# Moving the normed activations from 0 to 16 bytes modulo 64 in on-chip memory, in a two-layer decoder trunk

## The chip, the cores and the metric

The kernel runs on one core of one Trainium2 chip. The metric is the device time of one execution in microseconds (us). Three executions of the kernel before took 574.81, 575.57 and 575.68 us; the median is 575.57 us.

## What is computed

A sequence of 256 tokens with 1024 channels goes through one mLSTM layer, then shared keys and values are made from the stream, and then it goes through one attention layer with three branches. Cut to what matters here:

```python
h = rmsnorm(x, norm_pre[0])                       # hA in the kernel
xm, o_pre, z = split(h @ w_in, 3)                 # 1024 x 6144
... conv, block-diagonal q/k/v, gates, mlstm cell, head norm ...
x = x + rmsnorm(y @ a_w_out, norm_post[0])
kv = rmsnorm(x, kv_norm) @ kv_w                   # hK in the kernel
h = rmsnorm(x, norm_pre[1])                       # hB in the kernel
proj = h @ b_w_in                                 # 1024 x 8240: q, gates, three z branches
... compressed, selected and window attention, gated by silu(z) ...
x = x + rmsnorm(o @ b_w_out, norm_post[1])
```

All of it is float32.

## The kernel before

**Products in two parts.** A float32 product is made of two float32r parts per operand, `hi` and `lo` (`split`, L132: ScalarE copies to `hi`, VectorE subtracts to get `lo`). Each product is three matmuls (`mm3`, L137): L139 is hi by hi, L140 and L141 are the two mixed ones. A matmul of TensorE has a stationary operand of 128 columns, which a weight load (PEld) brings in beforehand, and a moving operand, which is streamed past it.

**Which operand moves.** In `proj_t` (L144) the weights `whi`/`wlo` are stationary and the normed activations `hA`, `hK` or `hB` move, 256 columns at a time; one call issues 2 x 8 x 3 = 48 matmuls into one PSUM tile. It makes `xmps` (L364 on), `zps`, `qps`, `xcps`, `ksps` and `kwps`; `branch_gates` (L784) makes `bgps` in the same way. In `o_gate` (L323) it is the other way round: `hA` is stationary and 512 columns of weights move. So it is in the values product of the keys/values stage (`vps`, L618), with `hK` stationary and `wv` moving, and in `OutProj.one` (L210), where the mixer's output (`y`, `ylow`, `yT`) is stationary and `whi`, `wlo` or `wl` moves.

**The order of the work.** Every engine works through its own program order. Weights come in chunks of 1024 elements per partition over the SyncE queue (`weights`, L115) into four rotating `raw` buffers and are split into five `whi` and four `wlo` buffers; the next chunks are loaded and split while TensorE works on the present one.

**The buffers that the change touches.** Pool `hp` has four buffers for tag `h8`. They hold in turn `hA` (hi and lo, `new_hT`, L193), the convolved activations `xc` (L320), two late weight chunks `wl` of the first output projection (`load_last`, L221), `hK`, `hB`, and the outputs `ylow` of the first three head pairs (L974). A tile starts where the allocator puts it, at a multiple of 32 bytes; a pool lies behind the one before it, and small `pad` tiles in the pools set where the next one starts. From the sizes and the order of the tiles, the start addresses of what TensorE reads, modulo 64 bytes, are these (slices of these tiles that the matmuls use start at multiples of 64 from there):

| operand | before | with the change |
|---|---|---|
| `hA`, `hK`, `hB` (hi and lo) | 0 | 16 |
| `xc` | 0 | 0 |
| `wl` (both) | 0 | 32 |
| `ylow` | 32 | 32 |
| `whi`, `wlo` | 32 | 32 |
| `y` of the first mixer, `yT`, `sd`, `v` of the cell | 32 | 32 |
| `wv`, `KT`, `V` | 0 | 0 |

Of the kernel before, what the change touches and what calls it, by code (L numbers as in the profile page):

```python
# [7 lines left out]
F32 = mybir.dt.float32  # L8
F32R = mybir.dt.float32r
# [6 lines left out]
P = 128  # L16
# [4 lines left out]
def trunk(ctx: ExitStack, tc: tile.TileContext, x, norm_pre, norm_post, a_w_in, a_conv_w, a_conv_b,  # L21
# [3 lines left out]
    S, D = x.shape[1], x.shape[2]  # L25
    NT = S // P
    KT = D // P
    AI = a_w_out.shape[1]
    AH = a_b_gate.shape[1] // 2
    ADH = AI // AH  # L30
    HT = ADH // P
# [11 lines left out]
    hp = ctx.enter_context(tc.tile_pool(name="hp", bufs=4))  # L43
# [53 lines left out]
    spare = []  # L97
# [81 lines left out]
    def norm_t(t, rstd, gam, hT):  # L179
# [10 lines left out]
            evac = split(hT[0][sl], hT[1][sl], ps)  # L190
        return ins.ins, *evac

    def new_hT(name):  # L193
        return [hp.tile([P, KT, S], F32R, tag="h8", name=f"{name}_{s}") for s in ("hi", "lo")]

    class OutProj:

# [22 lines left out]

        def load_last(self, k0, spare=0):  # L221

            homes = [[hp.tile([P, 2, 1024], F32R, tag="h8", name=f"wl{n}{k}") for n in range(2)] for k in range(0, spare, 2)]
            self.last = [(n, k, self.load(n, k, homes[(k - k0) // 2][n] if k < k0 + spare else None))
                         for k in range(k0, self.nk, 2) for n in range(2)]
            self.last.sort(key=lambda e: e[0])
# [19 lines left out]
    with ExitStack() as actx:  # L246
# [14 lines left out]
        nc.gpsimd.dma_start(out=rows[96:112], in_=a_skip[0].rearrange("(t p) -> t p", p=P))  # L261

        hT = new_hT("hA")
        keep_warm(8)
        gam_a = [wkt([P, 512], f"gam_a{n}") for n in range(2)]
# [51 lines left out]


        xm = [ah.tile([P, HT, S + 3], F32, tag="xm", name=f"xm{h}") for h in range(AH)]
        xc2 = [hp.tile([P, 2 * HT, S], F32, tag="h8", name=f"xc{h}") for h in range(AH // 2)]  # L320
        xc = [xc2[h // 2][:, h % 2 * HT:(h % 2 + 1) * HT, :] for h in range(AH)]
        for h in range(AH):
            nc.gpsimd.memset(xm[h][:, :, 0:3], 0.0)  # L323
# [40 lines left out]
        for j in range(NF // 2):  # L364
# [7 lines left out]
            h, j0 = divmod(2 * j, HT)  # L372
            nc.scalar.activation(xm[h][:, j0:j0 + 2, 3:], ps, AF.Copy)
            acc = a2.tile([P, 2, S], F32, tag="conv", name="conv")
            for m in range(2):
                f = 2 * j + m
# [211 lines left out]
        for c in range(4):  # L588
            n = wcount[0] = wcount[0] + 1
# [6 lines left out]
            vch.append([a.rearrange("p (k n) -> p k n", k=2) for a in hl])  # L596
        wv.tile([P, 120], F32, tag="pad", bufs=1, name="pad_wv")
        hK = new_hT("hK")
        rB, vps = [], []
        for t, n in op.finish():  # L600
            if n == 0:
                continue
            rB.append(rms_col(halves(xt[t])))
            with tc.high_priority(), tc.issue_after(op.near_end):
                ins = norm_t(t, rB[t], gam_k, hK)
            if t == 0:
                hold[:] = ins[2:]
            else:
                hold[:] = ins[0:2]
            vps.append(pjt([P, 512], f"vps{t}"))  # L610
            if t == 0:
                op_end = last_mm[0]
            with tc.issue_after(op_end):
                for c in range(4):
                    for k in range(2):
                        kk = 2 * c + k
                        mm3(vps[t], [a[:, kk, t * P:(t + 1) * P] for a in hK], [a[:, k, :] for a in vch[c]],
                            kk == 0, kk == KT - 1)  # L618
            if t == 0:
                hB = new_hT("hB")  # L620
            with tc.issue_after(last_mm[0]):
                norm_t(t, rB[t], gam_b, hB)
# [3 lines left out]
    with ExitStack() as bctx:  # L626
# [320 lines left out]
        def chunks(kv, c0, c1):  # L947
# [23 lines left out]
        pp = bctx.enter_context(tc.tile_pool(name="pp", bufs=7, side="right", reuse_waits="tile"))  # L971
        yp = bctx.enter_context(tc.tile_pool(name="yp", bufs=10, reuse_waits="tile"))
        yp.tile([P, 8], F32, tag="pad", bufs=1, name="pad_yT")
        ylow = [hp.tile([P, 4 * 2 * S], F32R, tag="h8", name=f"ylow{s}")[:, 56:56 + 3 * 2 * S].rearrange(  # L974
            "p (q i s) -> p q i s", q=3, i=2) for s in ("hi", "lo")]

        with tc.issue_after(after_norm):
# [58 lines left out]
```

## Time and profile before

| | |
|---|---|
| median of three executions | 575.57 us |
| the profiled execution, its own time | 574.73 us |
| its span from first to last instruction | 573.0 us |
| TensorE matmuls busy | 558.3 us (97%) |
| weight loads busy | 511.5 us (89%) |
| VectorE, ScalarE, GpSimd busy | 438.4, 316.8, 52.4 us |
| mean granted TensorE clock | 0.996 |

The profile is one execution. A matmul's own duration in it runs from its start to the modelled end of its passage through the array, and matmuls overlap; what one costs in a dense stream is therefore read from the distance between the starts of two that follow each other, over a run of many (starts are given to 0.01 us). Times are counted from the first instruction of the span.

### The profile page before, as it was taken

Reading aid. Unit: us, or ns where it says so; the run is one execution under the profiler, and the core shown is the slowest. Engines: PE = TensorE matmul, PEld = TensorE weight load, DVE = VectorE, ACT = ScalarE, POOL = GpSimd, SP = SyncE. Lnnn points to the kernel's source line nnn. Section 1 sums busy time; section 2 is a strip of 40 time slices with the busy share of each in tenths; the row PEclk is TensorE's granted clock in tenths of the full one; section 3 lists DMA queues with packets and bytes.
Section 4 is the critical chain, followed back from the end, with each engine's and each line's share of the span. In section 5 each row is a group of like instructions: output and inputs, shape, how many; then the busy total and the mean of one; then the engine's idle time right before and its main releaser. Section 6 shows DMA issues by size and latency. Waiting matters only on the chain.

```text
span 573.0 us, 10564 instructions
## 1 busy us (share of the span) xinstructions
PE 558.3 (97%) x4043; PEld 511.5 (89%) x4043; DVE 438.4 (77%) x927; ACT 316.8 (55%) x596; POOL 52.4 (9%) x88
## 2 busy tenths in 40 slices
PE   6999999999999999999999999999999999999995
PEld 2998987988999988879898999999999999998884
DVE  7679876485898876786625879888888888889563
ACT  6475777535544445464334766666666666666521
POOL 8623000101010040130000000000000000000000
PEclk9899999999999999999999999999999999999999
DMA  9995764253413447689996455555555545444501
GB/s 267 216 289 162 228 214 132 77 177 118 148 48 101 145 151 255 207 263 276 284 297 176 124 181 146 149 148 148 146 149 149 148 147 150 147 153 150 205 9 74
DMA packets 82693, 96.69 MB, mean 169 GB/s; under 512 B 4811, under 2 KB 68449, under 8 KB 82642
## 3 DMA queue, kind: packets, MB, share of 16 engines
q1 hardware_dynamic: 81040, 92.48, 52.9%
q0 software_dynamic: 1600, 3.52, 2.9%
q8 instruction: 32, 0.52, 0.4%
q14 instruction: 19, 0.16, 0.1%
q10 hardware_dynamic: 2, 0.00, 0.0%
HBM read 94.94 MB, written 1.05 MB: 168 GB/s over the span
## 4 chain that ended last, share of the span: by engine, by line
PE 84%; DMA 7%; DVE 4%; ACT 1%; issue 1%; SPq 1%; POOL 0%; DVEq 0%; POOLq 0%; ACTq 0%
PE zps L139 10%; PE zps L141 10%; PE zps L140 10%; PE acc L139 5%; PE acc L140 5%; PE acc L141 5%; DMA raw<-in_b_w_in_dram 4%; PE o L139 3%; PE o L140 2%; PE o L141 2%; PE xmps L141 2%; PE qps L139 2%; PE qps L141 2%; PE qps L140 2%; PE xmps L139 2%; PE xmps L140 2%
## 5 line engine op out<-in xcount | busy, mean ns | idle before, releaser
L135 DVE TENSOR_TENSOR wlo<-raw,whi 128x1024 fp32r<-128x1024 f32 x150 | 182.8, 1224 | 77.5 <-ACT whi L134 29.2
L134 ACT ACTIVATE whi<-raw 128x1024 fp32r<-128x1024 f32 x151 | 157.3, 1053 | 128.8 <-PE zps L140 28.2
L139 PE MATMUL zps<-hB_hi,whi 128*128 128x256 f32 x384 | 108.1, 282 | 0.0
L140 PE MATMUL zps<-hB_lo,whi 128*128 128x256 f32 x384 | 107.2, 279 | 0.0
L141 PE MATMUL zps<-hB_hi,wlo 128*128 128x256 f32 x384 | 107.1, 279 | 0.0
L139 PEld LDWEIGHTS zps<-hB_hi,whi 128*128 128x128 f32 x384 | 72.2, 188 | 0.8 <-ACT KThi L134 0.4
L140 PEld LDWEIGHTS zps<-hB_lo,whi 128*128 128x128 f32 x384 | 72.2, 188 | 0.0
L141 PEld LDWEIGHTS zps<-hB_hi,wlo 128*128 128x128 f32 x384 | 72.2, 188 | 0.0
L848 ACT ACTIVATE e<-e,nm 128x16 f32<-128x16 f32 (+2 forms) x96 | 38.0, 397 | 30.9 <-DVE nm L842 30.9
L141 PE MATMUL xmps<-hA_hi,wlo 128*128 128x256 f32 x128 | 36.8, 288 | 2.5 <-DVE wlo L135 2.5
L163 POOL TENSOR_TENSOR r<-u,mhalf 128x1 f32<-128x1 f32 x8 | 4.5, 562 | 350.8 <-DVE u L173 350.8
L139 PE MATMUL xmps<-hA_hi,whi 128*128 128x256 f32 x128 | 36.5, 285 | 0.0
L140 PE MATMUL xmps<-hA_lo,whi 128*128 128x256 f32 x128 | 36.4, 284 | 0.0
L139 PE MATMUL zps<-hA_hi,whi 128*128 128x256 f32 x128 | 36.1, 282 | 0.0
L141 PE MATMUL zps<-hA_hi,wlo 128*128 128x256 f32 x128 | 36.0, 281 | 0.0
L141 PE MATMUL qps<-hB_hi,wlo 128*128 128x256 f32 x128 | 35.7, 279 | 0.0
L139 PE MATMUL qps<-hB_hi,whi 128*128 128x256 f32 x128 | 35.7, 279 | 0.0
L140 PE MATMUL qps<-hB_lo,whi 128*128 128x256 f32 x128 | 35.7, 279 | 0.0
L140 PE MATMUL zps<-hA_lo,whi 128*128 128x256 f32 x128 | 35.7, 279 | 0.0
L141 PEld LDWEIGHTS xmps<-hA_hi,wlo 128*128 128x128 f32 x128 | 24.9, 194 | 2.9 <-DVE wlo L135 2.9
L381 DVE SCALAR_TENSOR_TENSOR conv<-xm,vec,conv 128x256 f32<-128x256 f32 x48 | 21.0, 479 | 6.3 <-ACT conv L378 6.2
L139 PE MATMUL o<-whi,hA_hi 128*128 128x512 f32 x64 | 25.6, 400 | 0.0
(337 smaller groups left out, 1397.9 us busy)
## 6 DMA issues: line engine op xcount, KB each, us to landing
raw<-in_b_w_in_dram SPq DMA_DIRECT2D x64, 512.0 KB, 4.9
raw<-in_a_w_in_dram SPq DMA_DIRECT2D x48, 512.0 KB, 4.7
raw<-in_a_w_out_dram SPq DMA_DIRECT2D x16, 512.0 KB, 3.5
w<-in_cmp_w_dram SPq DMA_DIRECT2D x32, 256.0 KB, 6.7
raw<-in_b_w_out_dram SPq DMA_DIRECT2D x16, 512.0 KB, 4.1
raw<-in_kv_w_dram SPq DMA_DIRECT2D x8, 512.0 KB, 5.8
raw<-in_kv_w_dram SPq DMA_DIRECT2D x8, 256.0 KB, 4.2
x<-in_x_dram SPq DMA_DIRECT2D x4, 256.0 KB, 3.7
```

The costliest lines, as they stand in the source:

```text
L134: a = nc.scalar.activation(hi, src, AF.Copy)
L135: return a.ins, nc.vector.tensor_sub(lo, src, hi.bitcast(F32)).ins
L139: nc.tensor.matmul(dst, lhsT=l[0], rhs=r[0], start=start, stop=False)
L140: nc.tensor.matmul(dst, lhsT=l[0], rhs=r[1], start=False, stop=False)
L141: last_mm[0] = nc.tensor.matmul(dst, lhsT=l[1], rhs=r[0], start=False, stop=stop).ins
L163: last_pow[0] = nc.gpsimd.tensor_tensor(r, u, mhalf[:, 0:n], op=ALU.pow)
L381: nc.vector.scalar_tensor_tensor(acc[:, m, :], src[:, k:k + S], vec[:, 16 * k + f:16 * k + f + 1], acc[:, m, :], op0=ALU.mult, op1=ALU.add)
L848: nc.scalar.activation(e[:, c0:c0 + n], e[:, c0:c0 + n], AF.Exp, bias=nm[:, i:i + 1], scale=-1.0, accum_out=sm[:, i:i + 1])
```

## The change

The four buffers get 16 float32 more (64 bytes), and each use takes its own place in them: the normed activations from element 4 (16 bytes), the late weight chunks from element 8 (32 bytes), `xc` from element 0 and `ylow` from element 56, as before. The second, third and fourth buffer thereby start 64, 128 and 192 bytes later, and all pools behind them on that side 256 bytes later, which leaves their addresses modulo 64 as they were. No instruction is added, removed or moved: on all five engines the order of instructions is the same before and after.

```diff
+    def buf8(name, dt):
+        return hp.tile([P, KT * S + 16], dt, tag="h8", name=name)
+
     def new_hT(name):
-        return [hp.tile([P, KT, S], F32R, tag="h8", name=f"{name}_{s}") for s in ("hi", "lo")]
+        return [buf8(f"{name}_{s}", F32R)[:, 4:4 + KT * S].rearrange("p (k s) -> p k s", k=KT) for s in ("hi", "lo")]
...
-            homes = [[hp.tile([P, 2, 1024], F32R, tag="h8", name=f"wl{n}{k}") for n in range(2)] for k in range(0, spare, 2)]
+            homes = [[buf8(f"wl{n}{k}", F32R)[:, 8:8 + 2048].rearrange("p (i n) -> p i n", i=2) for n in range(2)]
+                     for k in range(0, spare, 2)]
...
-        xc2 = [hp.tile([P, 2 * HT, S], F32, tag="h8", name=f"xc{h}") for h in range(AH // 2)]
+        xc2 = [buf8(f"xc{h}", F32)[:, 0:2 * HT * S].rearrange("p (j s) -> p j s", s=S) for h in range(AH // 2)]
...
-        ylow = [hp.tile([P, 4 * 2 * S], F32R, tag="h8", name=f"ylow{s}")[:, 56:56 + 3 * 2 * S].rearrange(
+        ylow = [buf8(f"ylow{s}", F32R)[:, 56:56 + 3 * 2 * S].rearrange(
             "p (q i s) -> p q i s", q=3, i=2) for s in ("hi", "lo")]
```

## Rows read from the trace of the kernel before

**Rows 1.** The page: busy time by engine, then the shares of the chain that ended last.

```profile
PE 558.3 (97%) x4043; PEld 511.5 (89%) x4043; DVE 438.4 (77%) x927; ACT 316.8 (55%) x596; POOL 52.4 (9%) x88
...
PE 84%; DMA 7%; DVE 4%; ACT 1%; issue 1%; SPq 1%; POOL 0%; DVEq 0%; POOLq 0%; ACTq 0%
```

**Rows 2.** TensorE's waits: who waited for whom, us in total, times, longest.

```profile
PE xmps L141 <- DVE wlo L135: 2.5, 2, 1.6
PE nT L188 <- DVE nrm L185: 2.0, 2, 1.1
```

**Rows 3.** Groups by line and shape: count, busy us, mean ns; L139 stands for L139 to L141.

```profile
L139 PE MATMUL zps<-hB_hi,whi 128*128 128x256 f32 x384 | 108.1, 282 | 0.0
...
L139 PE MATMUL xmps<-hA_hi,whi 128*128 128x256 f32 x128 | 36.5, 285 | 0.0
L139 PE MATMUL zps<-hA_hi,whi 128*128 128x256 f32 x128 | 36.1, 282 | 0.0
...
L139 PE MATMUL qps<-hB_hi,whi 128*128 128x256 f32 x128 | 35.7, 279 | 0.0
...
L139 PE MATMUL o<-whi,hA_hi 128*128 128x512 f32 x64 | 25.6, 400 | 0.0
...
L139 PE MATMUL xcps<-hK_hi,whi 128*128 128x256 f32 x32 | 9.0, 282 | 0.0
...
L139 PE MATMUL vps<-wvhi,hK_hi 128*128 128x512 f32 x16 | 6.3, 397 | 0.0
```

**Rows 4.** TensorE in order of time, one `proj_t` of the attention layer: start us, duration us.

```profile
339.28 0.28 PE L139 MATMUL zps<-hB_hi,whi 128*128 128x256 f32 x1
...
342.08 0.28 PE L139 MATMUL zps<-hB_hi,whi 128*128 128x256 f32 x1
```

**Rows 5.** The same view, `o_gate`: 512 columns of weights move, `hA` is stationary.

```profile
124.13 0.40 PE L139 MATMUL o<-whi,hA_hi 128*128 128x512 f32 x1
...
126.93 0.40 PE L139 MATMUL o<-whi,hA_hi 128*128 128x512 f32 x1
```

**Rows 6.** The same view, first output projection: weights in `whi`/`wlo`, then in `wl`.

```profile
228.97 0.39 PE L141 MATMUL acc<-whi,ylo 128*128 128x512 f32 x1
...
230.33 0.39 PE L141 MATMUL acc<-whi,ylo 128*128 128x512 f32 x1
230.56 0.40 PE L139 MATMUL acc<-wl,yhi 128*128 128x512 f32 x1
...
231.96 0.39 PE L139 MATMUL acc<-whi,yhi 128*128 128x512 f32 x1
```

**Rows 7.** The same view, second output projection and values product, 512 columns moving.

```profile
255.06 0.39 PE L139 MATMUL vps<-wvhi,hK_hi 128*128 128x512 f32 x1
...
257.10 0.39 PE L139 MATMUL vps<-wvhi,hK_hi 128*128 128x512 f32 x1
...
554.05 0.39 PE L139 MATMUL acc<-whi,yThi 128*128 128x512 f32 x1
...
565.61 0.39 PE L139 MATMUL acc<-whi,yThi 128*128 128x512 f32 x1
```

**Rows 8.** The same view: 12 transposes in one merged row; then their group, mean ns.

```profile
336.21 1.47 PE L873 MATMUL pt<-ident,e 128*128 128x128 f32 x12
...
L873 PE MATMUL pt<-ident,e 128*128 128x128 f32 x96 | 11.8, 273 | 0.0
```

**Rows 9.** The same view at the start, then busy time by stretch with the granted clock (PEclk).

```profile
15.51 0.41 PE L140 MATMUL xmps<-hA_lo,whi 128*128 128x256 f32 x1
...
18.07 0.41 PE L140 MATMUL xmps<-hA_lo,whi 128*128 128x256 f32 x1
...
core 0: us, PE busy (x) PEld busy (x) DVE busy (x) ACT busy (x) POOL busy (x), PEclk, DMA share, GB/s
15.50:18.00 2.50, 2.50 (x13) 2.50 (x13) 2.50 (x3) 0.30 (x1) 1.61 (x3) 0.50 1.18 69
```

**Rows 10.** Busy time by stretch, the same columns.

```profile
262.00:296.00 34.00, 34.00 (x333) 31.09 (x332) 16.73 (x17) 10.69 (x14) 0.00 (x0) 1.00 0.96 294
296.00:400.00 104.00, 103.53 (x892) 101.55 (x892) 82.25 (x217) 64.31 (x145) 0.00 (x0) 1.00 0.55 157
400.00:507.00 107.00, 107.00 (x890) 105.73 (x889) 92.83 (x256) 67.94 (x163) 0.00 (x0) 1.00 0.52 148
```

**Rows 11.** VectorE and ScalarE groups that write these buffers, and two on other places.

```profile
L135 DVE TENSOR_TENSOR ylo<-yt,yhi 128x512 fp32r<-128x512 f32 x8 | 5.4, 689 | 1.1 <-ACT yhi L134 0.9
L135 DVE TENSOR_TENSOR hB_lo<-nT,hB_hi 128x512 fp32r<-128x512 f32 x4 | 2.6, 680 | 0.0
L135 DVE TENSOR_TENSOR wl<-raw,wl 128x1024 fp32r<-128x1024 f32 x2 | 2.4, 1221 | 0.8 <-ACT wl L134 0.8
...
L134 ACT ACTIVATE yhi<-yt 128x512 fp32r<-128x512 f32 x8 | 4.9, 628 | 7.8 <-DVE yt L558 7.8
L134 ACT ACTIVATE hB_hi<-nT 128x512 fp32r<-128x512 f32 x4 | 2.3, 595 | 0.0
L134 ACT ACTIVATE wl<-raw 128x1024 fp32r<-128x1024 f32 x2 | 2.1, 1055 | 2.4 <-DMA raw<-in_a_w_out_dram 2.4
```

## The prediction

> **What bounds the kernel now.** I read the page first: TensorE's matmuls are busy for 97% of the span, and 84% of the chain that ended last is TensorE [rows 1]. Then its waits: the two longest sums are 2.5 and 2.0 us [rows 2]. So the span is a stream of matmuls with next to no holes in it, and its length is their number times the distance from one start to the next. The change leaves every instruction in its place; it can act only through that distance, or through the writes into the moved buffers. So the reader is to look at distances, by the kind of operands.
>
> *A product with the normed activations moving.* In one projection of the attention layer 24 matmuls lie between the starts at 339.28 and 342.08 us: 116.7 ns each, for 256 columns [rows 4]. Weights start at 32 modulo 64 there, activations at 0.
>
> [...]
>
> [...] In the first output projection, with the same stationary tiles and the same accumulators, six matmuls with weights in the rotating buffers (32 modulo 64, stationary y at 32) take 1.36 us, 226.7 ns each; the six behind them, whose weights lie in `wl` (0 modulo 64), take 1.40 us, 233.3 ns [rows 6]. The output gate, weights at 32 and stationary hA at 0, also takes 2.80 us for 12: 233.3 ns [rows 5]. The values product, both at 0, takes 2.04 us for 9: 226.7 ns, and the second output projection, both at 32, 11.56 us for 51: 226.7 ns [rows 7]. [...] A pair 16 bytes apart, which the change makes, is nowhere in this trace.
>
> **The change part by part.**
>
> *1. Projections, activations moving: 32 bytes apart becomes 16.* Three lines each of 384 + 128 + 128 + 128 + 32 matmuls [rows 3] make 2,400; `ksps` and `kwps` are one projection of 48 each and `bgps` 16: 2,512 in all, 293 us of the span at 116.7 ns. The price at 16 apart is not shown and is bounded. Below: every matmul here loads 128 new stationary columns, and 12 transposes that do no more than that for 128 moving columns take 1.47 us, the last of them 0.27: (1.47 - 0.27) / 11 = 109 ns apart [rows 8]. That is a floor: 2,512 x 7.7 = 19.3 us gained. [...] In between lies the price for equal places, half of 226.7, 113.3 ns: 8.4 us gained. I take the middle between the price at 0 apart (113.3) and at 32 apart (116.7), since 16 lies in the middle: 115.0 ns, a gain of 1.7 x 2,512 = 4.2 us.
>
> *2. Output gate, hA stationary: 192 matmuls, 32 apart becomes 16.* By the same middle 233.3 becomes 230.0: 0.6 us gained; bounds 0 to 1.3 gained (226.7), or the same 1.3 lost.
>
> *3. Values product, hK stationary: 48 matmuls, equal becomes 16 apart.* 226.7 becomes 230.0: 0.2 us lost; at 233.3 it is 0.3.
>
> *4. `wl` moving: 24 matmuls, 32 apart becomes equal.* 24 x 6.6 = 0.2 us gained; this one is measured on both sides [rows 6].
>
> *5. What cannot use the gain.* From 262 to 296 us the DMA engines are 96% busy [rows 10], with 256 of the 2,512 matmuls in it (xcps, ksps, kwps, bgps and the first q and z); weights set the pace there as soon as TensorE is quicker, so 0.4 us of part 1 is not had. Among the xm projections TensorE already waits 2.5 us for the lo split of the weights [rows 2]; I take half of their part (384 x 1.7 = 0.6) as lost, 0.3 us. In the attention stage the cover is there: VectorE is 79% busy from 296 to 400 us and 87% from 400 to 507 us [rows 10], ScalarE less, and a stream 1.4% shorter makes that 88% at most.
>
> *6. Writes and addresses.* Twelve evacuations each by ScalarE and VectorE write the moved activations. On a buffer at 0 they took 595 and 680 ns, the equal-sized ones of y at 32 628 and 689 ns [rows 11]: at most 33 ns by 12, 0.4 us, the lo parts 0.1 us; only those in the two norm stages are waited for, so I take 0 and keep 0.3 us for the range. The splits into `wl` (1055 and 1221 ns) are one-off and have TensorE's dense stream over them. The 64 and 192 bytes by which buffers move change addresses modulo 128 of half the tiles, `ylow` among them; no row separates that from modulo 64. Were `ylow`'s 72 matmuls to fall to 233.3, it would cost 0.5 us; I take 0.
>
> Sum: 4.2 + 0.6 - 0.2 + 0.2 - 0.7 = 4.1 us, so 574.73 becomes 570.6 for the profiled execution. That one stands 0.8 us below the median of three (575.57); between 570.6 and 571.5 I give **571.0 us**.
>
> [...] The rows say that where the two operands lie to each other is worth 6.6 ns on 512 columns. [...]
>
> **The rivals.**
>
> *A. No change (0.17): 575.2 us.* Only whether the two operands share a 32-byte place modulo 64 counts, and 16 apart costs what 32 apart costs. For: the trace knows two prices only. Parts 2 and 3 then give 0 and -0.3, part 4 +0.2. [...]
>
> *B. Slower (0.30): 583.5 us.* [...]
>
> *C. The whole gain (0.20, within "faster"): 566 us.* 16 apart is as good as equal or better: 113.3 ns, 8.4 + 1.3 + 0.2 = 9.9 us, less the uncovered part of it, about 1.4: 566.2. VectorE would then be 89% busy from 400 to 507 us, still not the bound. [...]
>
> **How the numbers follow.** Forecast (middle price) 0.33, C 0.20, A 0.17, B 0.30. About 0.2% (1.2 us) can be told from no change here; the cases lie on either side of that, so: faster 0.53, within 0.17, slower 0.30. Both signs hold much, and the range has to reach to C and to B: 562 to 584.5 us. What it leaves out is the floor price and a step larger than B's. The forecast's own range is 568 to 573.5 us (parts 1 and 2 between a third and two thirds of the way, part 6's 0.3 us and 0.8 us between execution and median).
>
> **What would show it.** Right: zps in the attention layer about 115 ns apart, the output gate at 230, acc from `wl` at 226.7, the values product at 230, the two output projections unchanged at 226.7, VectorE's share up by a point. Wrong: 116.7 again (A), 120 or more (B), 113 or less (C). A changed distance in acc with `whi` or in the second output projection would mean that more than these addresses counts; longer evacuations of hA, hK, hB, that the writes do; TensorE waiting for weights in the attention stage, that the gain was there and was taken by VectorE or the DMAs.

## The result, and the profile after

The kernel with the change takes 578.15 us (median of six executions, 577.79 to 579.17), the kernel before, beside it, 575.0 us (median of six). The ratio is 1.0061, 95% interval 1.0049 to 1.0072 (here and below the ratio is the one on record, which need not be the quotient of the two medians): slower by 3.2 us, against a forecast of 571.0, faster by 4. The profiled execution took 578.75 us with a span of 577.0, against 574.73 and 573.0.

The page of the kernel after, busy time by engine and then the shares of the chain that ended last, answers to [rows 1]:

```profile
PE 562.3 (97%) x4043; PEld 513.9 (89%) x4043; DVE 439.0 (76%) x927; ACT 316.6 (55%) x596; POOL 48.4 (8%) x88
...
PE 79%; DMA 9%; DVE 7%; ACT 2%; issue 1%; SPq 1%; POOL 0%; DVEq 0%; POOLq 0%; ACTq 0%
```

The same 4043 matmuls fill 97% of a longer span: 4.0 us more of busy TensorE, 4.0 us more of span. VectorE and ScalarE do the same work in the same time. The two waits that led before [rows 2]:

```profile
PE xmps L141 <- DVE wlo L135: 3.3, 5, 1.1
PE nT L188 <- DVE nrm L185: 1.9, 2, 1.2
```

They are no answer: the first is 0.8 us longer here, but in the slower kernels of this study it lies anywhere from 1.8 us (experiment 5, 578.86 us) to 3.6 (experiment 7, 580.88 us), and at 3.2 in the fastest (experiment 17, 574.2 us). Nor are the writes; the groups that answer to [rows 11]:

```profile
L135 DVE TENSOR_TENSOR hB_lo<-nT,hB_hi 128x512 fp32r<-128x512 f32 x4 | 2.6, 682 | 0.0
...
L134 ACT ACTIVATE hB_hi<-nT 128x512 fp32r<-128x512 f32 x4 | 2.3, 596 | 0.0
```

682 and 596 ns, where 680 and 595 stood. The stretch from 400 to 507 us has no hole, and fewer matmuls: 879, where [rows 10] had 890 in the same 107 us.

```profile
400.00:507.00 107.00, 107.00 (x879) 105.71 (x878) 92.01 (x253) 68.26 (x163) 0.00 (x0) 1.00 0.50 142
```

So the distance from matmul to matmul grew. TensorE in order of time (start us, duration us), the first and the last row of eight stretches of the kernel after:

```profile
110.17 0.28 PE L139 MATMUL zps<-hA_hi,whi 128*128 128x256 f32 x1
...
113.00 0.28 PE L139 MATMUL zps<-hA_hi,whi 128*128 128x256 f32 x1
...
124.55 0.40 PE L139 MATMUL o<-whi,hA_hi 128*128 128x512 f32 x1
...
127.33 0.40 PE L139 MATMUL o<-whi,hA_hi 128*128 128x512 f32 x1
...
227.76 0.39 PE L139 MATMUL acc<-wl,yhi 128*128 128x512 f32 x1
...
229.16 0.39 PE L139 MATMUL acc<-whi,yhi 128*128 128x512 f32 x1
...
231.90 0.39 PE L139 MATMUL acc<-wl,yhi 128*128 128x512 f32 x1
...
233.26 0.39 PE L139 MATMUL acc<-whi,yhi 128*128 128x512 f32 x1
...
254.89 0.39 PE L139 MATMUL vps<-wvhi,hK_hi 128*128 128x512 f32 x1
...
257.69 0.39 PE L139 MATMUL vps<-wvhi,hK_hi 128*128 128x512 f32 x1
...
340.72 0.28 PE L139 MATMUL zps<-hB_hi,whi 128*128 128x256 f32 x1
...
344.62 0.28 PE L139 MATMUL zps<-hB_hi,whi 128*128 128x256 f32 x1
...
530.15 0.39 PE L139 MATMUL acc<-whi,ylowhi 128*128 128x512 f32 x1
...
534.31 0.39 PE L139 MATMUL acc<-whi,ylowhi 128*128 128x512 f32 x1
...
558.07 0.39 PE L139 MATMUL acc<-whi,yThi 128*128 128x512 f32 x1
...
561.47 0.39 PE L139 MATMUL acc<-whi,yThi 128*128 128x512 f32 x1
```

| matmuls | in this stretch | ns apart | before | forecast |
|---|---|---|---|---|
| projections, hB moving | 33 in 3.90 us | 118.2 | 116.7 [rows 4] | 115.0 |
| projections, hA moving | 24 in 2.83 | 117.9 | 116.7 (45 in 5.25 from 108.45 us) | 115.0 |
| output gate, hA stationary | 12 in 2.78 | 231.7 | 233.3 [rows 5] | 230.0 |
| `wl` of the first column half | 6 in 1.40 | 233.3 | 233.3 [rows 6] | 226.7 |
| `wl` of the second | 6 in 1.36 | 226.7 | 233.3 | 226.7 |
| values product, hK stationary | 12 in 2.80 | 233.3 | 226.7 [rows 7] | 230.0 |
| output projection, `ylow` stationary | 18 in 4.16 | 231.1 | 226.7 (21 in 4.76 from 526.99 us) | 226.7 |
| output projection, `yT` stationary | 15 in 3.40 | 226.7 | 226.7 [rows 7] | 226.7 |

hB moves in 1,552 matmuls (3 x (384 + 128) for z and q, and 16 for `bgps`), hA in 768: 1,552 x 1.5 + 768 x 1.2 = 3.2 us lost. The 144 of `xcps` and `ksps`, hK moving, went from 116.7 to 117.8 ns, another 0.2 us. The small ones nearly cancel: `ylow` and the values product lose 0.3 us each, the output gate gains 0.3, `wl` 0.1. Sum 3.6 us, between the 3.2 of the medians and the 4.0 of the two spans.

Two of these rows say more than a size. The two `wl` halves now start at the same place modulo 64, and run at 233.3 and 226.7 ns. And `ylow`, whose address modulo 64 did not change at all, lost 4.4 ns. Modulo 64, in which the prediction counted, is too coarse. From the order and the sizes of the tiles the places are these, in bytes modulo 256: the weights `whi`, `wlo`, and `y`, `yT`, are at 224; before, every hi and lo part of hA, hK and hB was at 0 and both parts of `ylow` at 224. With the change a tile's hi and lo part lie in different buffers of the four, which start 64 bytes apart, so the two parts of each lie 64 apart modulo 128: at 16 and at 80. Modulo 256 the hi and the lo part of hA lie at 16 and 208, of hK at 16 and 80, and of hB, which moves in most of the matmuls, at 144 and 208. Of `ylow` the lo part stays with `y` modulo 128 and the hi part is 64 off; the first `wl` half is 64 off from `y` modulo 128, the second is level with it.

So the change had two parts that the prediction did not tell apart: the 16 bytes, and the 64 bytes of length that move the buffers and pull hi and lo apart.

### The profile page after: what moved, and what is told of

It reads as the page before. It is cut to its first block, busy times and chain, and to the rows that moved or that the text cites. A ratio compares the mean times of both kernels' runs of the same rounds, so it can differ in the third digit from the quotient of the medians.

```text
span 577.0 us, 10564 instructions
## 1 busy us (share of the span) xinstructions
PE 562.3 (97%) x4043; PEld 513.9 (89%) x4043; DVE 439.0 (76%) x927; ACT 316.6 (55%) x596; POOL 48.4 (8%) x88
## 3 DMA queue, kind: packets, MB, share of 16 engines
q0 software_dynamic: 1600, 3.52, 2.9%
## 4 chain that ended last, share of the span: by engine, by line
PE 79%; DMA 9%; DVE 7%; ACT 2%; issue 1%; SPq 1%; POOL 0%; DVEq 0%; POOLq 0%; ACTq 0%
PE zps L139 10%; PE zps L140 10%; PE zps L141 10%; PE acc L139 5%; PE acc L140 5%; PE acc L141 5%; DMA raw<-in_a_w_in_dram 3%; DMA raw<-in_b_w_in_dram 3%; PE qps L140 2%; PE qps L141 2%; PE qps L139 2%; PE o L139 2%; PE o L141 2%; PE o L140 2%; PE pt L877 2%; DVE wlo L135 2%
## 5 line engine op out<-in xcount | busy, mean ns | idle before, releaser
L139 PE MATMUL zps<-hB_hi,whi 128*128 128x256 f32 x384 | 108.2, 282 | 0.0
L141 PE MATMUL zps<-hB_hi,wlo 128*128 128x256 f32 x384 | 107.8, 281 | 0.0
L139 PEld LDWEIGHTS zps<-hB_hi,whi 128*128 128x128 f32 x384 | 72.6, 189 | 0.8 <-issue 0.4
L141 PEld LDWEIGHTS zps<-hB_hi,wlo 128*128 128x128 f32 x384 | 72.1, 188 | 0.0
L141 PE MATMUL xmps<-hA_hi,wlo 128*128 128x256 f32 x128 | 36.3, 284 | 3.3 <-DVE wlo L135 3.3
L139 PE MATMUL xmps<-hA_hi,whi 128*128 128x256 f32 x128 | 36.3, 284 | 0.3 <-ACT whi L134 0.2
L139 PE MATMUL zps<-hA_hi,whi 128*128 128x256 f32 x128 | 36.5, 285 | 0.0
L141 PE MATMUL qps<-hB_hi,wlo 128*128 128x256 f32 x128 | 36.0, 281 | 0.0
L141 PE MATMUL zps<-hA_hi,wlo 128*128 128x256 f32 x128 | 36.0, 281 | 0.0
L139 PE MATMUL qps<-hB_hi,whi 128*128 128x256 f32 x128 | 35.8, 279 | 0.0
L141 PEld LDWEIGHTS xmps<-hA_hi,wlo 128*128 128x128 f32 x128 | 24.0, 188 | 4.3 <-DVE wlo L135 4.3
L139 PE MATMUL o<-whi,hA_hi 128*128 128x512 f32 x64 | 25.6, 400 | 0.0
```

Of the source, the lines that this page charges most:

```text
L139: nc.tensor.matmul(dst, lhsT=l[0], rhs=r[0], start=start, stop=False)
L141: last_mm[0] = nc.tensor.matmul(dst, lhsT=l[1], rhs=r[0], start=False, stop=stop).ins
```

## The experiments

Diffs are against the kernel after, if nothing else is said, and some long lines end at `rearrange(`. "ns apart" is read as above, in the z projections of the attention layer (256 columns of hB moving), unless another product is named. Places are modulo 256, if nothing else is said. The "6.3%" of some expectations is over 213.3 ns for 512 columns, which is my estimate: 256 columns took 213.3 ns at a granted clock of 0.50 [rows 9], and I took the time as going with the number of columns and inversely with the clock. Of the weight load, which some expectations name, the trace of the kernel before gives this for the z projections of the attention layer: it takes 188 ns on average, longer than the 116.7 ns between two matmuls, and starts 0 to 0.01 us behind the matmul that runs beside it (339.17 us, the matmul at 339.16).

**1. The length without the 16 bytes.** Every use starts at element 0 of its longer buffer.

```diff
-        return [buf8(f"{name}_{s}", F32R)[:, 4:4 + KT * S].rearrange(
+        return [buf8(f"{name}_{s}", F32R)[:, 0:0 + KT * S].rearrange(
...
-            homes = [[buf8(f"wl{n}{k}", F32R)[:, 8:8 + 2048].rearrange(
+            homes = [[buf8(f"wl{n}{k}", F32R)[:, 0:0 + 2048].rearrange(
```

> Only the lengthening: the four buffers are 64 bytes longer, but the normed activations and the late weight chunks stay at element 0. Hi and lo tiles then lie 64 bytes apart modulo 128, everything stays as before modulo 64. Theory 1 (addresses count modulo 128, and the lengthening is what costs): projections of the attention layer at 118 ns instead of 116.7, the time 577 to 578.5 us, near the changed kernel. Theory 2 (the 16-byte start costs, the lengthening does not): 116.7 ns and 575 us, as before, but for the matmuls with ylow stationary, whose place is that of the changed kernel (231.5 ns instead of 226.7, 0.4 us).

578.03 us against 574.74: 1.0071 (1.0057 to 1.0085). TensorE in order of time in this kernel, hi and lo 64 apart:

```profile
411.87 0.29 PE L139 MATMUL zps<-hB_hi,whi 128*128 128x256 f32 x1
...
416.85 0.28 PE L139 MATMUL zps<-hB_hi,whi 128*128 128x256 f32 x1
```

42 in 4.98 us, 118.6 ns. Not one operand starts off a multiple of 32 bytes here, and the whole loss is there. The length is enough by itself. It puts hB at 128 (hi) and 192 (lo), hA at 0 and 192.

**2 to 4. Buffers of 128 bytes more, so that hi and lo agree modulo 128, with the activations at 16, 96 and 32 modulo 128.**

```diff
-    tp.tile([P, 72], F32, tag="pad", bufs=1, name="pad_h")
+    tp.tile([P, 8], F32, tag="pad", bufs=1, name="pad_h")
...
-        return hp.tile([P, KT * S + 16], dt, tag="h8", name=name)
+        return hp.tile([P, KT * S + 32], dt, tag="h8", name=name)
```

That alone is experiment 2, with the hi parts of the activations at 16 and the lo parts at 144; in 3 activations and `wl` start at element 24, in 4 the activations at 8 and `wl` at 24.

> Only the 16 bytes: buffers 128 bytes longer, so that every buffer starts at 0 modulo 128, normed activations at 16 modulo 128 in hi and lo alike; a pad before them is 256 bytes shorter to make room. Theory 1: the 16-byte start costs nothing, 115 to 116.7 ns, 571 to 575 us, ylow back at 226.7 ns. Theory 2: 118 ns and 577 to 578.5 us. If addresses count modulo 256 too, ylow stays near 231 ns, since its hi and lo tiles now lie 128 bytes apart modulo 256.

> Normed activations and late weight chunks at 96 modulo 128, the place of the weights, in every buffer. If 256 moving columns follow the same law as 512 (6.3% over at equal places): 113.3 ns, output gate 226.7, values product 233, late weight chunks 226.7, 565 to 567 us. If the weight load, which lasts through the whole of a 256-column matmul, makes equal places no better there: 116 ns or more, 574 to 580 us, with the output gate at 226.7 all the same. If modulo 256 counts, one of the two late weight chunks stays at 233.

> Normed activations at 32 modulo 128: equal to the weights modulo 64, 64 bytes apart modulo 128. A law modulo 64 gives what e3 gives, 113.3 ns and 566 us if that law holds for 256 columns. A law modulo 128 in which 64 apart costs what 32 apart costs, as the late weight chunks of the changed kernel show for 512 columns: 116.7 ns, output gate 233, 574 to 576 us.

At 16: 577.62 us, 1.0048 (1.0036 to 1.0061), 117.7 ns (39 in 4.59 us). At 96: 581.92, 1.0125 (1.0111 to 1.0139), 119.6 ns (27 in 3.23). At 32: 576.6, 1.0033 (1.002 to 1.0046), 117.1 ns (45 in 5.27). At 96 activations and weights agree modulo 128, and that is the slowest of the three, against every expectation built on equal places. And `ylow`, whose two parts agree modulo 128 and differ by 128 modulo 256, got slower still; the row view of experiment 2:

```profile
527.14 0.40 PE L139 MATMUL acc<-whi,ylowhi 128*128 128x512 f32 x1
...
533.44 0.39 PE L139 MATMUL acc<-whi,ylowhi 128*128 128x512 f32 x1
```

27 in 6.30 us, 233.3 ns, where before had 226.7. Modulo 128 does not do either.

**5 and 6. The 128 bytes with everything at 0; then the same buffers with the places put back.** Experiment 5 is experiment 2 with activations and `wl` at element 0: hi parts at 0, as in the kernel before, lo parts at 128. Experiment 6 starts the part of each tile that lies 128 bytes off 32 elements later (the lo part; of `ylow` the hi part), which makes good the 128 bytes. Its diff against experiment 5:

```diff
-        return [buf8(f"{name}_{s}", F32R)[:, 0:0 + KT * S].rearrange("p (k s) -> p k s", k=KT) for s in ("hi", "lo")]
+        return [buf8(f"{name}_{s}", F32R)[:, o:o + KT * S].rearrange("p (k s) -> p k s", k=KT) for s, o in (("hi", 0), ("lo", 32))]
...
-            homes = [[buf8(f"wl{n}{k}", F32R)[:, 0:0 + 2048].rearrange(
+            homes = [[buf8(f"wl{n}{k}", F32R)[:, 32 * n:32 * n + 2048].rearrange(
...
-        ylow = [buf8(f"ylow{s}", F32R)[:, 56:56 + 3 * 2 * S].rearrange(
+        ylow = [buf8(f"ylow{s}", F32R)[:, o:o + 3 * 2 * S].rearrange(
...
+            for s, o in (("hi", 88), ("lo", 56))]
```

> Buffers 128 bytes longer as in the run at 16, but the normed activations and late weight chunks at element 0: that run without its 16 bytes. Theory 1, now modulo 256 (what costs is that the hi and lo tiles no longer lie at the same place modulo 256): 117.6 to 118 ns in the attention layer's projections and 577 us, as there. Theory 2 (there the 16 bytes cost): 116.8 ns, 575 us.

> The same longer buffers, with the lo tiles (and the second late weight chunk, and ylow's hi tile) 128 bytes further into theirs, so that hi and lo lie at the same place modulo 256 again. Theory 1: back to 116.8 ns, ylow back to 227, 574.7 us although the buffers are longer. If addresses count modulo 512 too: the mLSTM projections, whose hi and lo agree modulo 512 here, are back at 116.8, those of the attention layer, 256 bytes apart modulo 512, stay at 117.6. Rival (the length or the shifted pads cost by themselves): 117.6 everywhere, 577 us.

Experiment 5: 578.86 us, 1.0061 (1.0037 to 1.0085), zps up to 118.7 ns (30 in 3.56 us), `ylow` 233.3 (21 in 4.90). Experiment 6: 574.79 us against 574.88, 0.9995 (0.9981 to 1.0008). Its rows:

```profile
410.93 0.28 PE L139 MATMUL zps<-hB_hi,whi 128*128 128x256 f32 x1
...
415.83 0.28 PE L139 MATMUL zps<-hB_hi,whi 128*128 128x256 f32 x1
...
527.21 0.39 PE L139 MATMUL acc<-whi,ylowhi 128*128 128x512 f32 x1
...
533.33 0.39 PE L139 MATMUL acc<-whi,ylowhi 128*128 128x512 f32 x1
```

42 in 4.90 us, 116.7 ns, and 27 in 6.12 us, 226.7 ns: both back where they were. The length itself costs nothing; what costs is the places modulo 256 that it gives the tiles. In experiment 5 only the lo parts had left 0, and yet the step from one matmul with a hi part moving to the next (L141 to L139) grew as well, from 116.7 to 117.9 ns on average in the z projections. How much of the loss is the place of the moved part and how much its distance from the other is not shown: with both parts at 128 (experiment 10) the price is 117.3 or 118.7 ns. In experiment 6 the parts of hA agree modulo 512 as well and those of hB and hK do not, and all are back, so 256 is enough.

**7 and 8. No longer buffers; all four buffers moved as one, to 224 (the weights' own place) and to 32.** The first diff is against the kernel before; for 32 the pad in `hp` has 8 elements, `pad_s` keeps 48, and `ylow` starts at 48.

```diff
-    sp.tile([P, 56], F32, tag="pad", bufs=1, name="pad_s")
+    hp.tile([P, 56], F32, tag="pad", bufs=1, name="pad_hp")
...
-        ylow = [hp.tile([P, 4 * 2 * S], F32R, tag="h8", name=f"ylow{s}")[:, 56:56 + 3 * 2 * S].rearrange(
+        ylow = [hp.tile([P, 4 * 2 * S], F32R, tag="h8", name=f"ylow{s}")[:, 0:0 + 3 * 2 * S].rearrange(
```

> Buffers as long as before, all four moved by 224 bytes (a pad goes from behind them to ahead of them), ylow's offset taken back: the normed activations lie at 224 modulo 256, exactly where the weights lie, hi and lo alike. The law of my forecast (equal places cost 6.3%): 113.3 ns, output gate 226.7, 565 to 567 us. Rival (at 256 columns the weight load runs through the whole matmul, and equal places collide): 119 ns or more, 578 us or more, with the output gate at 226.7 nevertheless.

> Buffers as long as before, all four moved by 32 bytes, ylow's offset taken back: the normed activations at 32 modulo 256, hi and lo alike. If only their common place counts, whatever it is: 116.8 ns, 574 to 575 us. If the distance from the weights (224, now 64 bytes away around 256 instead of 32) sets the price: another price, 113 to 120 ns, 566 to 583 us, the output gate moved too.

At 224: 580.88 us, 1.0094 (1.0071 to 1.0116). Its rows:

```profile
125.40 0.39 PE L139 MATMUL o<-whi,hA_hi 128*128 128x512 f32 x1
...
127.44 0.39 PE L139 MATMUL o<-whi,hA_hi 128*128 128x512 f32 x1
...
414.41 0.28 PE L139 MATMUL zps<-hB_hi,whi 128*128 128x256 f32 x1
...
416.93 0.28 PE L139 MATMUL zps<-hB_hi,whi 128*128 128x256 f32 x1
```

This pair of stretches refutes the prediction's step from 512 columns to 256. Equal places give the output gate its 226.7 ns (9 in 2.04 us; 228.2 on average over the whole gate), as [rows 7] promised for 512 columns; and the same equal places give 256 columns 120.0 ns (21 in 2.52 us), not the 113.3 that is half of it, and worse than the 116.7 at 32 apart. At 32 everywhere: 576.52 us, 1.0025 (1.001 to 1.004), 117.8 ns (45 in 5.30), but one projection ran 42 matmuls in 4.76 us from 433.85 us on, 113.3 ns; the output gate stayed at 233.3, which the second theory had moving.

**9. The 16 bytes without any split.** Buffers of 256 bytes more keep hi and lo at one place; activations at 16, the late weight chunks at 224 like `y`, all other operands where they were modulo 256.

```diff
-    tp.tile([P, 72], F32, tag="pad", bufs=1, name="pad_h")
-    sp.tile([P, 56], F32, tag="pad", bufs=1, name="pad_s")
+    tp.tile([P, 8], F32, tag="pad", bufs=1, name="pad_h")
...
-        return hp.tile([P, KT * S + 16], dt, tag="h8", name=name)
+        return hp.tile([P, KT * S + 64], dt, tag="h8", name=name)
...
-            homes = [[buf8(f"wl{n}{k}", F32R)[:, 8:8 + 2048].rearrange(
+            homes = [[buf8(f"wl{n}{k}", F32R)[:, 56:56 + 2048].rearrange(
...
-        ap.tile([P, 104], F32, name="pad_y")
+        ap.tile([P, 32], F32, name="pad_y")
...
+        bp.tile([P, 56], F32, name="pad_b")
```

> The 16 bytes alone: buffers 256 bytes longer, so that all four start at 0 modulo 256, normed activations at 16 modulo 256 in hi and lo alike, late weight chunks at 224 (equal to the y tiles); pads elsewhere shortened so that all other places modulo 256 stay. If the split of hi and lo by 64 bytes is the whole loss of the changed kernel: 116.8 ns, 574.5 to 575.5 us. If the 16 bytes cost too: 117.5 ns or more, 576 us or more. My forecast's middle price would be 115 ns, 570.5 us.

578.12 us against 574.32: 1.0063 (1.0049 to 1.0077). Its rows:

```profile
412.84 0.28 PE L139 MATMUL zps<-hB_hi,whi 128*128 128x256 f32 x1
...
416.75 0.28 PE L139 MATMUL zps<-hB_hi,whi 128*128 128x256 f32 x1
```

33 in 3.91 us, 118.5 ns. So the 16 bytes alone cost what the length alone costs, and both together (578.15) no more than either. Together they put hB at 144 and 208, a place of neither experiment, so there was no sum to expect. The output gate, with both parts of hA at 16:

```profile
124.09 0.40 PE L139 MATMUL o<-whi,hA_hi 128*128 128x512 f32 x1
...
126.89 0.40 PE L139 MATMUL o<-whi,hA_hi 128*128 128x512 f32 x1
```

12 in 2.80 us, 233.3 ns, the price before: for the gate the 16 bytes bring nothing. The values product, with hK at 16, ran one of its two halves at 226.7 ns and the other at 233.3.

**10 to 16 and 18. Other places in the family of experiment 9.** Only the element at which hA, hK and hB start differs (4 there). Each ran once, so their times are compared only by whole microseconds; the distances are read from the trace. The kernel before took 574.32 us beside 9 to 12, 575.04 (one run) beside 13 to 16 and 574.99 beside 18.

> The same with the activations at 128 modulo 256, 96 bytes below the weights at 224. If every place but the weights' own costs the same: 116.8 to 117.7 ns, 574 to 577 us. If the price falls with distance: below 116.7 ns, 566 to 573 us.

> The same at 192 modulo 256, 32 bytes below the weights, where the kernel before lies 32 bytes above them (0 against 224). If only the size of the distance counts: 116.8 ns, 575 us. If its sign counts, since the weight load starts a few ns behind the matmul: another price, 113 to 120 ns, 566 to 583 us.

> The same at 240 modulo 256, 16 bytes above the weights: between the equal place (120.0 ns) and 32 above (116.8). A price that falls evenly with distance: 118.4 ns, 579 us. If a start off a multiple of 32 costs: over 120 ns, 583 us or more.

> Activations at 248 modulo 256, 24 bytes above the weights, hi and lo alike. At 240 a projection ran at one of three steady distances (113.3, 116.7, 118.7 ns). Theory 3 (the distance of the places sets which rhythms exist, and what ran before picks one): other rhythms than at 240, 113.3 to 118.7 ns, 566 to 579 us. [...]

> The same at 232, 8 bytes above the weights, near the equal place with its one rhythm of 120.0 ns. [...]

> The same at 208, 16 bytes below the weights: the distance of 240 with the other sign. If the sign does not count: 113.3 to 118.7 ns in a mixture, 575 to 578 us. If it does, as between 192 (118.1) and 0 (116.8): one rhythm, 117 to 120 ns, 576 to 581 us.

> [...]

> All normed activations at 216 modulo 256, 8 bytes below the weights: 16 below gave 117.1 ns with the output gate at 228.3, 0 gave 120.0, 8 above a mixture of 117.6 and 120.0. A price that moves evenly: 118.5 ns, output gate 227.5, 577 us. If the rhythm of 113.3 is the only one here: 566 to 568 us.

"Behind" is at a higher address than the weights, "ahead" at a lower one, counted around 256.

| experiment | activations at | from the weights (224) | us | ns apart |
|---|---|---|---|---|
| (before) | 0 | 32 behind | 575.0 | 116.7 |
| 9 | 16 | 48 behind | 578.12 | 118.5 |
| 8 | 32 | 64 behind | 576.52 | 117.8, once 113.3 |
| 10 | 128 | 96 ahead | 578.05 | 117.3 or 118.7 |
| 11 | 192 | 32 ahead | 578.48 | 118.1 |
| 15 | 208 | 16 ahead | 574.32 | 117.3 |
| 18 | 216 | 8 ahead | 581.62 | 120.0 |
| 7 | 224 | equal | 580.88 | 120.0 |
| 14 | 232 | 8 behind | 576.5 | 117.6 or 120.0 |
| 16 | 236 | 12 behind | 576.68 | 117.6 |
| 12 | 240 | 16 behind | 577.61 | 113.3, 116.7 or 118.7 |
| 13 | 248 | 24 behind | 582.07 | 120.0 |

Neither the distance from the weights nor its sign orders this list: 8 ahead, equal and 24 behind share the worst price, and 16 ahead is nearly as good as 32 behind. Experiment 18 was a plain miss: no theory that I had gave its 120.0 ns; the times of 10, 12, 13 and 15 lay outside what was expected too. The step of 8 bytes from 208 (experiment 15, first two rows) to 216 (experiment 18):

```profile
410.90 0.28 PE L139 MATMUL zps<-hB_hi,whi 128*128 128x256 f32 x1
...
414.42 0.28 PE L139 MATMUL zps<-hB_hi,whi 128*128 128x256 f32 x1
...
410.87 0.28 PE L139 MATMUL zps<-hB_hi,whi 128*128 128x256 f32 x1
...
413.39 0.28 PE L139 MATMUL zps<-hB_hi,whi 128*128 128x256 f32 x1
```

30 in 3.52 us and 21 in 2.52, 117.3 and 120.0 ns. The output gate averages 228.4 ns at 208, as low as at the equal place (228.2), and 233.3 at 216. Experiment 12 holds three prices in one execution; its rows:

```profile
142.39 0.28 PE L139 MATMUL zps<-hA_hi,whi 128*128 128x256 f32 x1
...
147.49 0.28 PE L139 MATMUL zps<-hA_hi,whi 128*128 128x256 f32 x1
...
164.95 0.28 PE L139 MATMUL zps<-hA_hi,whi 128*128 128x256 f32 x1
...
169.50 0.28 PE L139 MATMUL zps<-hA_hi,whi 128*128 128x256 f32 x1
...
383.91 0.28 PE L139 MATMUL zps<-hB_hi,whi 128*128 128x256 f32 x1
...
388.90 0.28 PE L139 MATMUL zps<-hB_hi,whi 128*128 128x256 f32 x1
```

45 in 5.10 us, 39 in 4.55 and 42 in 4.99: 113.3, 116.7 and 118.8 ns, the same operands at the same places each time. A projection falls into one steady distance and keeps it.

**17. A place for each tile: hA at 208, hK and hB at 0.** As experiment 9, with

```diff
-        return [buf8(f"{name}_{s}", F32R)[:, 4:4 + KT * S].rearrange("p (k s) -> p k s", k=KT) for s in ("hi", "lo")]
+        return [buf8(f"{name}_{s}", F32R)[:, 52 * (name == "hA"):52 * (name == "hA") + KT * S].rearrange(
+            "p (k s) -> p k s", k=KT) for s in ("hi", "lo")]
```

> Put together from the places read so far: hA alone at 208 modulo 256, where the output gate took 228.3 ns instead of 233.4 and the projections 117.1 instead of 116.9; hK and hB at 0 as before; late weight chunks at 224. 192 x 5.1 = 1.0 us and 24 x 7 = 0.2 us gained, 768 x 0.2 = 0.2 us lost: 573.9 us against 574.9, 0.2% faster than the kernel before. Theory 3 holds if hB and hK are back at 116.7 ns beside it; if places were tied across tiles, hB would leave 116.7.

574.2 us against 574.99: 0.9986 (0.9974 to 0.9998), 0.8 us less than the kernel before, close to the expected 573.9 and barely clear of no change. Its rows:

```profile
123.32 0.39 PE L139 MATMUL o<-whi,hA_hi 128*128 128x512 f32 x1
...
126.75 0.39 PE L139 MATMUL o<-whi,hA_hi 128*128 128x512 f32 x1
...
410.87 0.28 PE L139 MATMUL zps<-hB_hi,whi 128*128 128x256 f32 x1
...
415.07 0.28 PE L139 MATMUL zps<-hB_hi,whi 128*128 128x256 f32 x1
```

The output gate runs at 228.7 ns (15 in 3.43 us), 4.6 less than before on 192 matmuls, 0.9 us; hB at 0 is back at 116.7 (36 in 4.20). A tile's place prices the products that read it, and leaves the others alone.

## Why the prediction was wrong

**What held.** TensorE's stream is the bound and nothing covers it: matmuls times the change of their distance give 3.6 us, where 3.2 to 4.0 us were lost. The edit acts through addresses alone; writes cost nothing (682 and 596 ns beside 680 and 595, part 6), neither VectorE (439.0 us busy beside 438.4) nor the weights took a part, the output projection from `yT` stayed at 226.7. One half of `wl` came to 226.7 (part 4, 0.1 for 0.2).

**What came out by luck.** The output gate did gain (part 2, 0.3 us of the 0.6) and the values product did lose (part 3, 0.3 for 0.2), but not by a middle price at 16. With both parts of hA at 16 the gate takes 233.3 ns, no gain, and the values product with hK at 16 keeps 226.7 in one half (experiment 9). In the changed kernel the lo part of hA lies at 208 and that of hK at 80, which the prediction did not count; at 208 the gate averages 228.4 ns (experiment 15).

**The step that failed is part 1,** 4.2 us gained, measured as 3.4 us lost on hA, hB and hK. Three things in it were wrong, each with its run.

*Half the price of 512 columns was taken for that of 256.* "In between lies the price for equal places, half of 226.7, 113.3 ns": experiment 7 has equal places at both widths, 226.7 ns at 512 and 120.0 at 256. I built that step on one agreement of two numbers: at 32 apart, 116.7 ns and 233.3 ns are both 9.4% over an estimate of mine, 106.7 ns for 256 columns (half of the 213.3 ns at a granted clock of 0.50 [rows 9]) and 213.3 ns for 512. No run shows the estimate as a price; the lowest read for these products are 113.3 and 226.7 ns. At the equal place the two widths go opposite ways; at 208 both are near their best (117.3 and, on average, 228.4 ns).

*A middle was taken where there is no scale.* At 16, 48 bytes behind the weights modulo 256, the price is 118.5 ns with hi and lo together (experiment 9): outside the two prices that it was put between. Between 208 and 248, steps of 4 to 16 bytes go 117.3, 120.0, 120.0, 117.6 or 120.0, 117.6, 113.3 to 118.8, 120.0. The nearest rows bounded nothing here, and "16 lies in the middle" was no reason.

*Addresses were counted modulo 64, and the lengthening put at 0* ("no row separates that from modulo 64; ... I take 0", part 6). Modulo 256 counts: experiment 1 loses all of it by length alone, experiments 2 and 5 show 128 bytes to matter, experiment 6 that 256 are enough. What I weighed there was the address of `ylow` (0.5 us at most; 0.3 came); what I didn't see is that a length which is no multiple of 256 gives the hi and the lo part of the *same* activation different places, in all 2,512 matmuls of part 1.

**The rivals.** A, no change, fell. B forecast the side that came. Its 583.5 us, like the 120 ns that was to show it, comes from 3.3 ns more on each of the 2,512 matmuls, for a start that is no multiple of 32. No run shows that term: in the changed kernel at most 1.5 ns came, experiments 1 and 5 lose as much with every start on 32, and experiment 12, with a start off 32, has stretches at 113.3 ns. C fell with part 1, though its 113.3 ns exists, in single projections of experiments 8 and 12.

**What the places cost.** The rows give 113.3 to 120.0 ns for one and the same matmul by where its operands start. With the activations at 16 instead of 0 the time is 0.6% longer (experiment 9), and a move of 8 bytes, from 208 to 216, takes the distance from 117.3 to 120.0 ns (experiments 15 and 18).

**What stays open.** That the loss comes from the places modulo 256 is shown (experiments 1, 5 and 6). Why a place is dear is not: no run shows what gives each place its price, nor what picks one of the distances where there are several. The rival of experiment 7, by which equal places collide, forecast 119 ns or more, and 120.0 came; but experiments 13 and 18 have 120.0 ns without equal places, and no run shows a collision.

## What to carry to other kernels

Where a dense stream of float32r matmuls is the bound, treat the start addresses of the operands modulo 256 as a parameter of the kernel, like a tile size: here a per cent hangs on them (574.2 to 582.07 us), no busy share shows it (TensorE 97% before and after), and only the distance between starts does. Keep rotating buffers a multiple of 256 bytes long, so that every tile keeps its place when one of them is moved, and read the change of every tile's address before costing an edit as a move of one. Then try places instead of interpolating between them, at each width of the moving operand, and give each tile its own (experiment 17).

## What the runs showed that I had not expected

- The address counts modulo 256 (experiments 5 and 6) and by steps as small as 8 bytes (experiments 15 and 18), with prices for 256 columns from 113.3 to 120.0 ns.
- Equal places of the two operands are among the best at 512 moving columns (226.7 ns) and the worst at 256 (120.0, as at 216 and 248).
- At some places a projection settles into one of several distances and keeps it: 113.3, 116.7 and 118.8 ns in one execution. The clean ones are 113.3, 116.7 and 120.0 ns, at even steps of 3.3 to 3.4 ns.
